# Attention product of two heads as one 512-column operand, and a later transpose step, in an encoder kernel on Trainium2

## Chip, cores, metric

One core of a Trainium2 chip runs the whole program in one launch. The metric is device time in microseconds (us). Three runs of the kernel before took 2294.6, 2294.95 and 2295.01 us, median 2294.95 us.

## What is computed

The reference is a two-layer encoder on 256 positions of width 2048, in float32. Layer 0 mixes tokens with mixer A, layer 1 with mixer B (dilated windows); each is followed by a gated MLP with a width-3 convolution. Everything that the change touches is in mixer A:

```python
qkv = h @ w_qkv                                   # h: 256 x 2048, RMS-normed
q = axial_rope(rms_norm(q, q_gain))               # 16 heads of 128
k = axial_rope(rms_norm(k, k_gain))               #  4 heads of 128
logits = einsum('bqkgd,bskd->bkgqs', q, k) * 128 ** -0.5
p = softmax(logits)
o = einsum('bkgqs,bskd->bqkgd', p, v)             # 4 query heads share one k/v head
return o @ w_o
```

## The kernel before

**Numbers.** Almost every product is made of three matmuls with fp32r operands. A float32 value is split into a high part, `hi`, and a rest, `lo`, and `mm3` (L205 to 212) adds hi by hi (L210), lo by hi (L211) and hi by lo (L212). `split` (L192 to 197) makes the pair: ScalarE (ACT) copies into `hi` (L196), VectorE (DVE) subtracts into `lo` (L197). Weights are split as they arrive: `wh` on ACT (L156), `wl` on DVE (L157), in tiles of 1024 columns.

**Projections and steps.** `project` computes a 512-column block of `h @ w` as four calls of `feed`, one for each 512 rows of the weight. A feed loads its weights over the SP queue (L134), and has two halves; each half has one cast `wh`, one cast `wl` and two k-tiles, and each k-tile issues six 512-column matmuls (L144 to 146). Work that belongs to an earlier block is hung in between as Python generators in the list `pending`. `feed` calls `step` after each k-tile: after the first of a half it goes on only with a generator that stopped at `yield "half"`, after the second with the first generator of the list. So one step of a generator is spent for each half of a feed, 8 for each `project`. The engine queues keep, for the most part, the order in which this Python code issues instructions, but the tool that schedules them takes whatever it reckons to be ready, and the weight casts run in a region of raised priority (`AHEAD`), ahead of their place.

**Mixer A.** First `project2` makes the k and v blocks. Then, for g = 0 to 3, `project` makes the q block of four heads and `start(attend(g, accs))` hangs in its attention, which runs during the next `project` (for g = 3 during `out_proj`). `attend` runs in this order:

- `qk_post` (L581): ACT copies the block to `s` (tile `stg`, L477) and squares it into `sq` (L591), GpSimd (POOL) makes the rotary half `t2` in four instructions (L597); one step later DVE multiplies by the cosines (L600), and at the next one adds `t2` into `ro` (L602), sums the squares (L603), and POOL takes the root (L273, tile `rqk`).
- one step later `heads_T` issues eight TensorE (PE) transposes of `ro` (L494) and two splits into `qT`.
- then k = 0 to 5, each a step in two parts around `yield "half"`. First part, for k < 4: the product of q and k of head k (six 256-column matmuls into a PSUM tile), its maximum (L646), the scaling of the maximum (L648), two exponentials on ACT (L652), a reciprocal (L655), and the scaling of the probabilities on POOL (L656, tile `pr`). Second part, for k = 1 to 4: four transposes of the probabilities of head k-1 (L665) and their split into `pTh`, `pTl`. Behind it, for k = 2 to 5: the product with v of head k-2, two k-tiles by three matmuls of 256 columns, and its split into the slot of the head (`ah`, `al`).

Tiles with the same tag share memory. `rp` and `gbs`, the rotary table and the two gains (loaded at L522 and L525, read by POOL at L530 and L534 for `ct` and `st`), lie in the buffers of `pTh` and `pTl`, which have two each.

`out_proj` runs `project2` over `w_ao`: the first three feeds of two column blocks, then `drain()`, then the last feed of each. The last feeds read the slots of g = 3.

Of the kernel before, what the change touches and what calls it, by code (L numbers as in the profile page):

```python
# [7 lines left out]
F32 = mybir.dt.float32  # L8
F32R = mybir.dt.float32r
# [4 lines left out]
P = 128  # L14
D = 2048
NT = 256
# [12 lines left out]
def tile_encoder(ctx: ExitStack, tc: tile.TileContext, x, xT, w_a, w_ao, q_gain, k_gain, w_b, w_bo,  # L29
# [26 lines left out]
    def nm(s):  # L56
        uid[0] += 1
        return f"{s}_{uid[0]}"

    def ps_tile():  # L60
        return psp.tile([P, 512], F32, tag="ps", name=nm("ps"))
# [3 lines left out]
    def copy(o, i):  # L65
        turn[0] ^= 1
        if turn[0]:
            nc.scalar.activation(o, i, AF.Copy)
        else:
            nc.vector.tensor_copy(o, i)  # L70
# [121 lines left out]
    def split(hi, lo, src):  # L192
        if lo is None:
            copy(hi, src)
            return
        nc.scalar.activation(hi, src, AF.Copy)  # L196
        nc.vector.tensor_tensor(lo, src, hi.bitcast(F32), ALU.subtract)  # L197
# [7 lines left out]
    def mm3(o, lhsT, rhs, ls, rs, start, stop):  # L205
        (lh, ll), (rh, rl) = lhsT, rhs
        if ll is None:
            nc.tensor.matmul(o, lh[ls], rh[rs], start=start, stop=stop)  # L208
            return
        nc.tensor.matmul(o, lh[ls], rh[rs], start=start, stop=False)  # L210
        nc.tensor.matmul(o, lh[ls], rl[rs], start=False, stop=False)  # L211
        nc.tensor.matmul(o, ll[ls], rh[rs], start=False, stop=stop)  # L212

    def pair_tile(pool, shape, tag, bufs=1, whole=False):
        if whole:
            return pool.tile(shape, F32, tag=tag + "h", name=nm(tag), bufs=bufs), None
        return tuple(pool.tile(shape, F32R, tag=tag + c, name=nm(tag + c), bufs=bufs) for c in "hl")
# [9 lines left out]
    def new_slots(kts):  # L227
        return {kt: new_slot(kt) for kt in kts}
# [251 lines left out]
    def evac_split(pool, accs, rstd, whole=False):  # L480
        hi, lo = pair_tile(pool, [P, 2, 512], "v", 1, whole)
        for m in range(2):
            split_scaled(hi[:, m, :], lo if lo is None else lo[:, m, :], accs[m], rstd[:, m:m + 1])
        return hi, lo

    def heads_T(o, s):
        for hp in range(2):
            if hp:
                yield
            t = ps_tile()  # L490
            for j in range(2):
                for m in range(2):
                    i = 2 * hp + j
                    nc.tensor.transpose(t[:, j * NT + m * P:j * NT + (m + 1) * P],  # L494
                                        s[:, m, i * P:(i + 1) * P], ident)
            hi, lo = (v[:, 2 * hp:2 * hp + 2, :].rearrange("p a c -> p (a c)") for v in o)
            split(hi, lo, t)
# [12 lines left out]
    def mixer_a():  # L510
        with tc.tile_pool(name="apool", bufs=1) as ap:
# [1 line left out]
            hT, ss_in = {}, new_ss()  # L513
            kgs = list(range(4))

            rp = ap.tile([P, 2, 2, P], F32, tag="pTh", name="rp", bufs=2)
            gbs = ap.tile([P, 4, P], F32, tag="pTl", name="gbs", bufs=2)
            tabs = {}
            rstd = []

# [61 lines left out]
            def qk_post(accs, which, keep, scale=1.0):  # L582
                s = evac_scaled(ap, accs, rstd[0], 1)
                ct, st = tabs[which]
                ssq = small.tile([P, 8], F32, tag="ssq", name=nm("ssq"))
                r = small.tile([P, 8], F32, tag="rqk", name=nm("rqk"), bufs=3)
                ro = ap.tile([P, 2, 512], F32, tag="ro", name=nm("ro"))
                t2 = ap.tile([P, 2, 512], F32, tag="t2", name=nm("t2"))
                sq = ap.tile([P, 2, 512], F32, tag="sq", name=nm("sq"))
                for m in range(2):  # L590
                    nc.scalar.activation(sq[:, m, :], accs[m], AF.Square, scale=rstd[0][:, m:m + 1])  # L591
                rv, sv = (t.rearrange("p m (a c) -> p m a c", a=4) for t in (ro, s))
                for m in range(2):
                    t5, s5 = (t[:, m, :].rearrange("p (a f e c) -> p a f e c", a=4, f=2, e=2) for t in (t2, s))
                    st5 = st[:, m, :].rearrange("p (f e c) -> p f e c", f=2, e=2)
                    for e in range(2):
                        nc.gpsimd.tensor_tensor(t5[:, :, :, e, :], s5[:, :, :, 1 - e, :],  # L597
                                                st5[:, None, :, e, :].to_broadcast([P, 4, 2, 32]), ALU.mult)
                yield
                nc.vector.tensor_tensor(rv, sv, ct[:, :, None, :].to_broadcast([P, 2, 4, P]), ALU.mult)  # L600
                yield
                nc.vector.tensor_tensor(ro, ro, t2, ALU.add)  # L602
                nc.vector.tensor_reduce(ssq, sq.rearrange("p m (a c) -> p (m a) c", a=4), axis=AX.X, op=ALU.add)  # L603
                rsqrt_mean(r, ssq, P * scale * scale, EPS / (scale * scale))
                keep.extend((ro, r))

            slots = new_slots(range(16))
# [15 lines left out]
            v = evac_split(ap, va, rstd[0])  # L623
# [3 lines left out]
            def attend(g, accs):  # L627
                keep = []
                yield from qk_post(accs, "q", keep, SCALE)
                ro, rq = keep  # L630
                rqv = rq.rearrange("p (m a) -> p m a", m=2)
                qT = pair_tile(ap, [P, 4, NT], "qT")
                yield
                for _ in heads_T(qT, ro):
                    pass
                prs, pTs, ots = {}, {}, {}
                for k in range(6):
                    yield
                    if k < 4:
                        i = k  # L640
                        s = ps_tile()
                        for m in range(2):
                            mm3(s[:, m * NT:(m + 1) * NT], qT, kT,
                                (slice(None), i, slice(m * P, (m + 1) * P)), (slice(None), g), True, True)
                        mx = small.tile([P, 2], F32, tag="mx", name=nm("mx"), bufs=3)
                        nc.vector.tensor_reduce(mx, s.rearrange("p (m c) -> p m c", m=2), axis=AX.X,  # L646
                                                op=ALU.max, negate=True)
                        nc.vector.tensor_tensor(mx, mx, rqv[:, :, i], ALU.mult)  # L648
                        pr = ap.tile([P, 2, NT], F32, tag="pr", name=nm("pr"), bufs=2)
                        l = small.tile([P, 2], F32, tag="l", name=nm("l"), bufs=3)  # L650
                        for m in range(2):
                            nc.scalar.activation(pr[:, m, :], s[:, m * NT:(m + 1) * NT], AF.Exp,  # L652
                                                 bias=mx[:, m:m + 1], scale=rq[:, 4 * m + i:4 * m + i + 1],
                                                 accum_out=l[:, m:m + 1])
                        nc.vector.reciprocal(l, l)  # L655
                        nc.gpsimd.tensor_tensor(pr, pr, l[:, :, None].to_broadcast([P, 2, NT]), ALU.mult)  # L656
                        prs[i] = pr
                    yield "half"
                    if 1 <= k < 5:
                        i = k - 1  # L660
                        pr = prs.pop(i)
                        t = ps_tile()
                        for m in range(2):
                            for kt in range(2):
                                nc.tensor.transpose(t[:, kt * NT + m * P:kt * NT + (m + 1) * P],  # L665
                                                    pr[:, m, kt * P:(kt + 1) * P], ident)
                        pTs[i] = pair_tile(ap, [P, 2 * NT], "pT", 2)
                        split(pTs[i][0], pTs[i][1], t)
                    if k >= 2:
                        i = k - 2  # L670
                        pT = pTs.pop(i)
                        ot = ps_tile()[:, :NT]
                        for kt in range(2):
                            mm3(ot, v, pT, (slice(None), kt, slice(g * P, (g + 1) * P)),
                                (slice(None), slice(kt * NT, (kt + 1) * NT)), kt == 0, kt == 1)
                        hi, lo = slots[4 * g + i]
                        split(hi, lo, ot)

            for g in range(4):
                start(attend(g, project(w_a, g, hT, kgs)))  # L680
# [258 lines left out]
```

## Time and profile before

| what | us |
|---|---|
| runs, median of three | 2294.95 |
| the profiled execution, its own time | 2294.99 |
| span of the profile (first to last instruction) | 2293.2 |
| PE busy | 2280.3 |
| DVE busy | 1631.3 |
| ACT busy | 1218.1 |
| POOL busy | 170.3 |

The busy time of PE counts a matmul to its modelled end, so that consecutive matmuls overlap; what a matmul costs is read from the distance between the starts of neighbours. `PEld` are PE's weight loads, which run beside the matmuls. In the timeline a row has the start, the duration, engine, line, operation, output and inputs, and in brackets the idle time of the engine before it and what ended it; consecutive alike instructions are merged into one row with their count. A row that ends in `x4` is thus four instructions.

### The profile page before, as it was taken

What the parts mean: (1) busy time and instruction counts of PE and PEld (TensorE: products, weight loads), DVE (VectorE), ACT (ScalarE), POOL (GpSimd) and SP (SyncE); (2) the same over time, 40 slices, a digit from 0 to 9 for tenths busy, and PEclk for the clock granted to TensorE, in tenths of its full rate; (3) what the DMA queues carried; (4) which work ended last, traced back from release to release, by engine and by line L of the source; (5) the groups of instructions that cost most, each with busy time, mean ns of one, the idle gap of its engine ahead of it and who ended that gap; (6) DMA issues with size and microseconds to landing.
All of it is one profiled execution on the core that took longest, in us unless ns stands there. A gap on an engine that the chain in (4) does not pass through costs nothing.

```text
span 2293.2 us, 31100 instructions
## 1 busy us (share of the span) xinstructions
PE 2280.3 (99%) x11641; PEld 1947.1 (85%) x11641; DVE 1631.3 (71%) x2284; ACT 1218.1 (53%) x1746; POOL 170.3 (7%) x170
## 2 busy tenths in 40 slices
PE   9999999999999999999999999999999999999998
PEld 7888888888888888888888888888888888888886
DVE  6877877776457776878866875676777744777754
ACT  7565565554345555545454554445555533555543
POOL 2331101110000000010000000000000000000010
PEclk9999999999999999999999999999999999999999
DMA  8535656765555555566555554566555565555554
GB/s 299 166 131 164 202 190 206 214 213 194 194 194 184 192 190 189 188 216 210 185 175 181 178 189 163 178 198 206 189 189 189 188 194 193 191 190 187 192 191 149
DMA packets 261447, 437.57 MB, mean 191 GB/s; under 512 B 17216, under 2 KB 198208, under 8 KB 261168
## 3 DMA queue, kind: packets, MB, share of 16 engines
q1 hardware_dynamic: 254912, 425.64, 56.6%
q0 software_dynamic: 5952, 9.38, 1.6%
q8 instruction: 91, 1.49, 0.3%
q10 hardware_dynamic: 432, 0.56, 0.1%
q14 instruction: 60, 0.49, 0.1%
HBM read 429.20 MB, written 6.29 MB: 190 GB/s over the span
## 4 chain that ended last, share of the span: by engine, by line
PE 97%; DVE 1%; DMA 0%; issue 0%; POOL 0%; ACT 0%; SPq 0%; POOLq 0%; DVEq 0%; ACTq 0%
PE acc L123 28%; PE acc L145 17%; PE acc L146 17%; PE acc L144 17%; PE acc L121 15%; PE ps L208 1%; PE ps L211 1%; PE ps L212 0%; PE ps L210 0%; DMA raw<-in_w_a_dram 0%; DVE wl L157 0%; PE ps L665 0%; PE ps L815 0%; DVE tT L237 0%; POOL t L597 0%
## 5 line engine op out<-in xcount | busy, mean ns | idle before, releaser
L157 DVE TENSOR_TENSOR wl<-raw,wh 128x1024 fp32r<-128x1024 f32 (+1 forms) x456 | 553.5, 1216 | 320.1 <-ACT wh L156 316.2
L156 ACT ACTIVATE wh<-raw 128x1024 fp32r<-128x1024 f32 (+1 forms) x456 | 475.0, 1045 | 514.5 <-PE acc L146 449.6
L123 PE MATMUL acc<-xh,wh 128*128 128x512 f32 x2816 | 674.2, 391 | 0.0
L123 PEld LDWEIGHTS acc<-xh,wh 128*128 128x128 f32 x2816 | 517.0, 188 | 99.9 <-DVE v L356 0.4
L112 DVE TENSOR_TENSOR wl<-raw,wh 128x1024 fp32r<-128x1024 f32 x352 | 457.9, 1301 | 196.6 <-ACT wh L111 196.6
L111 ACT ACTIVATE wh<-raw 128x1024 fp32r<-128x1024 f32 x352 | 372.0, 1058 | 208.4 <-issue 70.9
L144 PE MATMUL acc<-wh,ah 128*128 128x512 f32 x1024 | 399.3, 390 | 0.0
L145 PE MATMUL acc<-wl,ah 128*128 128x512 f32 x1024 | 398.8, 389 | 0.0
L146 PE MATMUL acc<-wh,al 128*128 128x512 f32 x1024 | 398.7, 389 | 0.0
L121 PEld LDWEIGHTS acc<-xh,wl 128*128 128x128 f32 x2816 | 361.8, 191 | 14.2
L121 PE MATMUL acc<-xh,wl 128*128 128x256 f32 x2816 | 366.7, 283 | 0.0
L144 PE MATMUL acc<-wh,xh 128*128 128x512 f32 x768 | 302.7, 395 | 1.9 <-ACT wh L156 1.9
L145 PE MATMUL acc<-wl,xh 128*128 128x512 f32 x768 | 300.0, 391 | 0.2 <-DVE wl L157 0.2
L146 PE MATMUL acc<-wh,xh 128*128 128x512 f32 x768 | 299.8, 390 | 0.0
L146 PEld LDWEIGHTS acc<-wh,al 128*128 128x128 f32 x1024 | 192.2, 188 | 40.0
L144 PEld LDWEIGHTS acc<-wh,ah 128*128 128x128 f32 x1024 | 192.3, 188 | 39.4
L145 PEld LDWEIGHTS acc<-wl,ah 128*128 128x128 f32 x1024 | 192.3, 188 | 39.3
L146 PEld LDWEIGHTS acc<-wh,xh 128*128 128x128 f32 x768 | 144.2, 188 | 30.4
L144 PEld LDWEIGHTS acc<-wh,xh 128*128 128x128 f32 x768 | 144.4, 188 | 30.0 <-ACT wh L156 2.3
L145 PEld LDWEIGHTS acc<-wl,xh 128*128 128x128 f32 x768 | 144.4, 188 | 27.8 <-DVE wl L157 0.5
L375 POOL TENSOR_TENSOR cv<-cg,cv 128x512 f32<-128x512 f32 x44 | 63.5, 1444 | 1101.9 <-DVE cv L367 1101.9
L355 ACT ACTIVATE v<-acc 128x256 f32<-128x256 f32 x176 | 65.8, 374 | 108.5 <-PE acc L123 108.5
(156 smaller groups left out, 1385.8 us busy)
## 6 DMA issues: line engine op xcount, KB each, us to landing
raw<-in_w_up_dram SPq DMA_DIRECT2D x352, 512.0 KB, 3.7
raw<-in_w_down_dram SPq DMA_DIRECT2D x176, 512.0 KB, 3.6
raw<-in_w_b_dram SPq DMA_DIRECT2D x144, 512.0 KB, 3.8
raw<-in_w_bo_dram SPq DMA_DIRECT2D x48, 512.0 KB, 3.6
raw<-in_w_a_dram SPq DMA_DIRECT2D x40, 512.0 KB, 4.3
raw<-in_w_ao_dram SPq DMA_DIRECT2D x32, 512.0 KB, 3.7
raw<-in_w_a_dram SPq DMA_DIRECT2D x16, 256.0 KB, 6.1
h<-in_x_dram SPq DMA_DIRECT2D x4, 512.0 KB, 7.9
```

The lines of the kernel that those rows point to most:

```text
L111: nc.scalar.activation(wh, rk, AF.Copy)
L112: nc.vector.tensor_tensor(wl, rk, wh.bitcast(F32), ALU.subtract)
L121: nc.tensor.matmul(acc[j][:, :NT], wl[:, kt, c], lhs[4 * kg + kt][0], start=st, stop=sp)
L123: nc.tensor.matmul(acc[j], wh[:, kt, c], lhs[4 * kg + kt][2], start=st, stop=sp)
L144: nc.tensor.matmul(accs[m], xh[:, c], wh[:, j, :], start=st, stop=False)
L145: nc.tensor.matmul(accs[m], xh[:, c], wl[:, j, :], start=False, stop=False)
L146: nc.tensor.matmul(accs[m], xl[:, c], wh[:, j, :], start=False, stop=sp)
L156: nc.scalar.activation(wh[:, c], r[:, c], AF.Copy)
L157: nc.vector.tensor_tensor(wl[:, c], r[:, c], wh[:, c].bitcast(F32), ALU.subtract)
L208: nc.tensor.matmul(o, lh[ls], rh[rs], start=start, stop=stop)
L355: nc.scalar.activation(v[:, j], acc[j][:, NT:], AF.Copy)
L375: nc.gpsimd.tensor_tensor(cv, cg, cv, ALU.mult)
```

## The change

Three things are changed in mixer A.

- The product with v is taken for two heads at a time. `pTh` and `pTl` become one tile of 128 x 2 x 2 x 256 for a pair of heads (one buffer each instead of two), head by head in the inner index, so that a k-tile of both heads is one operand of 512 columns. The product of heads 0 and 1 is issued at k = 3 and that of heads 2 and 3 at k = 5, ahead of that step's transposes, where it was behind them at k = 2 to 5. The two results are split one after the other.
- `attend(0)` has one more `yield` in front of `heads_T`.
- `rp` lies in the buffer of `sq`; `gbs` in the now single buffer of `pTl`.

```diff
-            rp = ap.tile([P, 2, 2, P], F32, tag="pTh", name="rp", bufs=2)
-            gbs = ap.tile([P, 4, P], F32, tag="pTl", name="gbs", bufs=2)
+            rp = ap.tile([P, 2, 2, P], F32, tag="sq", name="rp")
+            gbs = ap.tile([P, 4, P], F32, tag="pTl", name="gbs")
...
                 qT = pair_tile(ap, [P, 4, NT], "qT")
                 yield
+                if g == 0:
+                    yield
                 for _ in heads_T(qT, ro):
                     pass
-                prs, pTs, ots = {}, {}, {}
+                prs, pTs = {}, {}
...
                     yield "half"
+                    if k in (3, 5):
+                        i = k - 3
+                        pT = [p.rearrange("p k a c -> p k (a c)") for p in pTs.pop(i // 2)]
+                        ot = ps_tile()
+                        for kt in range(2):
+                            mm3(ot, v, pT, (slice(None), kt, slice(g * P, (g + 1) * P)),
+                                (slice(None), kt), kt == 0, kt == 1)
+                        for j in range(2):
+                            split(*slots[4 * g + i + j], ot[:, j * NT:(j + 1) * NT])
                     if 1 <= k < 5:
...
-                        pTs[i] = pair_tile(ap, [P, 2 * NT], "pT", 2)
-                        split(pTs[i][0], pTs[i][1], t)
-                    if k >= 2:
-                        i = k - 2
-                        pT = pTs.pop(i)
-                        ot = ps_tile()[:, :NT]
-                        for kt in range(2):
-                            mm3(ot, v, pT, (slice(None), kt, slice(g * P, (g + 1) * P)),
-                                (slice(None), slice(kt * NT, (kt + 1) * NT)), kt == 0, kt == 1)
-                        hi, lo = slots[4 * g + i]
-                        split(hi, lo, ot)
+                        if i % 2 == 0:
+                            pTs[i // 2] = [ap.tile([P, 2, 2, NT], F32R, tag="pT" + c, name=nm("pT" + c))
+                                           for c in "hl"]
+                        split(*(p[:, :, i % 2, :] for p in pTs[i // 2]), t.rearrange("p (k c) -> p k c", k=2))
```

## The prediction

> **What bounds the kernel now.** I read the page first: shares of the engines, the granted clock, the chain.
>
> ```profile
> span 2293.2 us, 31100 instructions
> PE 2280.3 (99%) x11641; PEld 1947.1 (85%) x11641; DVE 1631.3 (71%) x2284; ACT 1218.1 (53%) x1746; POOL 170.3 (7%) x170
> PEclk9999999999999999999999999999999999999999
> PE 97%; DVE 1%; DMA 0%; issue 0%; POOL 0%; ACT 0%; SPq 0%; POOLq 0%; DVEq 0%; ACTq 0%
> ```
>
> PE is the bound from end to end, at the full clock, and idle for only 12.9 us (2293.2 - 2280.3). The profiled execution took 2294.99 us, 1.8 us more than its span and 0.04 us more than the median of the runs; my sum is made against 2294.99.
>
> Next the busy times by stretch: from the k block's attention work to the end of mixer A's q blocks. The first column is the stretch, the second its length, the third PE busy with its count.
>
> ```profile
> 0.00:46.30 46.30, 42.77 (x181) 34.62 (x182) 29.04 (x45) 32.67 (x59) 9.32 (x24) 1.00 0.92 322
> 46.30:73.30 27.00, 27.00 (x121) 22.36 (x120) 24.10 (x34) 13.99 (x16) 6.49 (x5) 1.00 0.57 183
> 73.30:103.40 30.10, 29.53 (x157) 24.92 (x156) 23.96 (x34) 19.42 (x38) 11.17 (x8) 1.00 0.56 180
> 103.40:133.90 30.50, 30.50 (x169) 25.96 (x169) 23.18 (x34) 19.38 (x39) 10.46 (x9) 1.00 0.43 140
> 164.50:200.00 35.50, 35.50 (x196) 30.08 (x195) 25.84 (x38) 22.37 (x42) 11.51 (x10) 1.00 0.42 136
> ```
>
> The attention runs between about 82 and 200 us. In all of it PE stands still once, for 0.57 us (30.10 - 29.53). So there is little to win from waits; what else the change can win must come from matmuls becoming cheaper or fewer. Since DVE (24 of 30 us) and ACT (19 of 30) are well filled, what it can lose is a wait that it opens.
>
> **The one wait.** The timeline around it, PE first, then DVE and POOL, which set it:
>
> ```profile
> 71.68 0.39 PE L146 MATMUL acc<-wh,xh 128*128 128x512 f32 x1
> ...
> 81.88 0.39 PE L146 MATMUL acc<-wh,xh 128*128 128x512 f32 x1
> 82.84 1.09 PE L494 MATMUL ps<-ident,ro 128*128 128x128 f32 x8 [0.57 <-DVE ro L602]
> 83.69 0.47 PE L144 MATMUL acc<-wh,xh 128*128 128x512 f32 x1
> ...
> 75.06 5.51 POOL L597 TENSOR_TENSOR t<-stg,st_q 128x256 f32<-128x256 f32 x4 [16.66 <-ACT stg L477]
> 78.63 3.02 DVE L157 TENSOR_TENSOR wl<-raw,wh 128x1024 fp32r<-128x1024 f32 x2
> 81.57 1.21 DVE L602 TENSOR_TENSOR ro<-ro,t 128x1024 f32<-128x1024 f32 x1
> 85.06 1.27 DVE L197 TENSOR_TENSOR qTl<-ps,qTh 128x512 fp32r<-128x512 f32 x2
> 86.54 0.28 PE L210 MATMUL ps<-kTh,qTh 128*128 128x256 f32 x1
> ```
>
> From 71.68 to 81.88 lie 45 matmuls of 512 columns, 0.227 us apart. The first q block's transposes then start 0.96 us after their neighbour, 0.73 more than that: they wait for `ro`, ready at 82.78. PE loses 0.73 us here (the bracket counts 0.57, since it counts the neighbour to its modelled end).
>
> With the extra yield in `attend(0)` the transposes come half a feed later: 12 matmuls, 2.7 us, so at 82.11 + 2.7 = 84.8 us. `ro` is then 2.0 us old. **Gain 0.73 us**; bounds 0 (if the DVE subtraction of two tiles, 3.02 us, slides once more in front of L602) and 0.73. What is late next: both `qTl` end at 86.33, and the first q by k product starts at 86.54. All of that moves along with the transposes, so it keeps its distance of a half feed. The sums and the small root on POOL (L273) and the casts of weights stay where they were and are covered by the same matmuls. The extra step moves no DMA. Every later step of all four attentions comes one half feed later, g = 1 to 3 because `attend(g)` is served only when `attend(g-1)` has ended.
>
> **The product with v.** One product as it stands without transposes in front of it, and one behind transposes:
>
> ```profile
> 96.04 0.60 PE L665 MATMUL ps<-ident,pr 128*128 128x128 f32 x4
> 96.39 0.36 PE L210 MATMUL ps<-pTh,vh 128*128 128x256 f32 x1
> 96.59 0.28 PE L211 MATMUL ps<-pTl,vh 128*128 128x256 f32 x1
> ...
> 97.19 0.39 PE L144 MATMUL acc<-wh,xh 128*128 128x512 f32 x1
> 98.58 0.28 PE L210 MATMUL ps<-kTh,qTh 128*128 128x256 f32 x1
> ...
> 108.56 0.28 PE L210 MATMUL ps<-pTh,vh 128*128 128x256 f32 x1
> ...
> 109.28 0.39 PE L144 MATMUL acc<-wh,xh 128*128 128x512 f32 x1
> ```
>
> From 108.56 to 109.28 six matmuls of 256 columns take 0.72 us, 0.120 each. Behind transposes the six take 0.80 (96.39 to 97.19); the first is 0.20 instead of 0.12 long. That 0.08 us belongs to the change from transposes to products: at 83.69, where a projection follows transposes, its first matmul is longer by as much (0.47 modelled against the 0.39 of its like). The number of such changes stays (16 transposes of probabilities, each followed by something), so nothing is won or lost there.
>
> A pair of heads costs 12 x 0.120 = 1.44 us before. After, six matmuls of 512 columns: at 0.227 (the quiet rows above) 1.36 us, at the 0.232 of the six between 97.19 and 98.58, 1.39 us. Eight pairs: gain 0.64 or 0.40 us. I take 0.5, between them, as the new matmuls lie amid attention, nearer to the second. The columns streamed are the same; what goes is 48 matmuls and 48 weight loads, with about 0.012 us of overhead each. **Gain 0.5 us.**
>
> The Trainium skill has a lower value for this term: in "TensorE: Matmul & The Clock Gate", section "Back-to-back issue gap", a warm matmul of N columns costs N/2.4 + 2.5 ns alone. By that, as an estimate from its figures, two of 256 columns cost 218.3 ns and one of 512 215.8, so 48 merged pairs would win only 0.12 us, and the sum would be about 2293.9. The trace does not agree: its rows say 0.120 and 0.227 us, and they decide.
>
> **The rest of the merge.** The splits of probabilities write 256 of every 512 columns, and the two results are split at k = 3 and 5 instead of one at each of k = 2 to 5: same number and width, all on ACT and DVE. I cost them at nothing, since what needs them comes late: a `pTl` that ends at 102.70 (`102.01` below) goes with a product behind the transposes of 104.60, 2.3 us later, and a pair's second `pTl` keeps this distance of half a feed. With one buffer the split of head 2 must wait until the pair's product has read the tile, but the transposes that it waits for anyhow stand behind that product on PE. Were the cover gone, one `pTl` split late would cost its 0.69 us, at most, for each of eight pairs.
>
> `rp` in the buffer of `sq` puts a wait in front of the first `sq` on ACT, with the `wh` casts behind it. It has long been met:
>
> ```profile
> 29.43 0.77 POOL L534 TENSOR_TENSOR st_q<-rp,gbs 128x64 f32<-128x64 f32 x1
> ...
> 48.48 1.26 ACT L591 ACTIVATE sq<-acc,rstd 128x512 f32<-128x512 f32 x2
> ```
>
> The last reader ends at 30.2, `sq` is first written at 48.5. The loads of `rp` and `gbs` keep their place on the SP queue and write a buffer nobody used before them. Cost 0.
>
> **What moves over a block's end.** This is where a new wait could come. Now the end of block 1 (about 103.2 us) falls behind the last head's q by k product; after, that product is the first thing behind the end, since all is half a feed later. The rows of head 3 and of the next block's start:
>
> ```profile
> 99.18 0.28 PE L212 MATMUL ps<-kTh,qTl 128*128 128x256 f32 x1
> ...
> 104.60 0.66 PE L665 MATMUL ps<-ident,pr 128*128 128x128 f32 x4
> ...
> 100.10 1.21 DVE L157 TENSOR_TENSOR wl<-raw,wh 128x1024 fp32r<-128x1024 f32 x1
> 102.01 0.69 DVE L197 TENSOR_TENSOR pTl<-ps,pTh 128x512 fp32r<-128x512 f32 x1 [0.62 <-ACT pTh L196]
> 104.53 1.78 DVE L600 TENSOR_TENSOR ro<-stg,ct_q 128x1024 f32<-128x1024 f32 x1 [0.73 <-ACT stg L477]
> ...
> 103.50 1.04 POOL L656 TENSOR_TENSOR pr<-pr,l 128x512 f32<-128x512 f32 x1 [3.73 <-PE acc L146]
> 104.50 3.80 POOL L597 TENSOR_TENSOR t<-stg,st_q 128x256 f32<-128x256 f32 x4
> ...
> 103.22 1.28 ACT L477 ACTIVATE stg<-acc,rstd 128x512 f32<-128x512 f32 x2
> ```
>
> From the end of the q by k product (99.30) to the scaled probabilities (103.50 + 1.04 = 104.54) the chain of head 3 takes 5.24 us, and its transposes start at 104.60: just in time, even a little late, as four take 0.66 instead of 0.60 us. After the change, counted from the block's end T: product of head 3 0.72, k-tile 1.38 (the six above), product of heads 0 and 1 1.38, transposes of head 2 0.44, k-tile 1.38, k-tile 1.38: the transposes of head 3 start at T + 6.68, their probabilities are ready at T + 0.72 + 5.24 = T + 5.96. Slack 0.7 instead of none. Head 2's transposes start behind the pair's product at T + 3.48; its q by k product ended at T - 3.2 (two k-tiles and one set of transposes before T), so it is ready at T + 2.0. Heads 0 and 1 keep the gaps that they have. So the small delays of the last head go: **gain 0.06 a block, 0.2 us in all**, bounds 0 and 0.3.
>
> In `out_proj`, attention of g = 3 ends in the first k-tile of the sixth feed, ahead of `drain`; its last slots are read two k-tiles into the seventh, five k-tiles (6.9 us) later. Cost 0.
>
> **The sum.** 0.73 + 0.5 + 0.2 = 1.4 us less: 2294.99 - 1.4 = 2293.6 us. Its own bounds are the least of each term (0 + 0.4 + 0) and the most (0.73 + 0.64 + 0.3): 2294.6 and 2293.3.
>
> **Rivals.**
>
> *POOL's order at the block's end (slower).* The four `t2` instructions of the next block (3.80 us on POOL) become ready at T + 0.75, when ACT has copied the first half (1.28 for two). The scaling of head 2's probabilities becomes ready at about T + 0.9, one `pr` (1.04) ahead of T + 2.0. If the four stand first in POOL's queue, it starts at T + 4.55, ends at T + 5.6, and PE's transposes at T + 3.48 wait 2.1 us, three times (there is no next block after g = 3): 6.4 us, so 2293.6 + 6.4 = 2300.0. It decides from the second `t2` ahead: one (0.95) still ends at T + 2.9. For it: the schedule takes what is ready, and now `t2` follows L656 at once (104.50). Against it: head 2's scaling is issued half a feed earlier and is reckoned ready at the same time. 5%.
>
> *DVE's order there.* If the multiplication L600 (1.78 us) slips into head 3's chain beside the cast (1.21) that is in it already, head 3 is ready at T + 7.74, 1.06 late, three times 3.2 us: 2296.8. For it: DVE takes L600 as soon as `stg` is there (104.53). Against: the maximum's scaling has precedence once it is ready. 13%.
>
> *The steady pitch.* The matmuls of a projection amid attention go at up to 0.232 against 0.227 us. If small matmuls cause that, fewer of them could free up to half of 0.005 us on about 370 matmuls, 0.9 us more: 2292.7. For it, the two rows; against, the transposes and the q by k products stay. 9%.
>
> *The change doesn't do what it says.* The merged matmul costs twice 0.120 us after all, as nothing here shows a 512-column one with `pTh` as input: 2293.6 + 0.5 = 2294.1; or the wait for `ro` only moves along: 2293.6 + 0.73 = 2294.3. Against it, 0.232 is the longest distance that the rows of 512 columns show without a switch. 10%. The formula of the Trainium skill's page that is named above points to the first of the two.
>
> **How the numbers follow.** The forecast has 61%, the rest is as above, with 2% for something unseen, as much up as down. A change within 0.2% (4.6 us) is about what a measurement of this kernel can't tell from none. Forecast, pitch, no gain and DVE's order all lie within it: 61 + 9 + 10 + 13 = 93%. Slower by more needs POOL's order or the unseen: 6%. Faster by more would need over three times all that the trace shows to be had: 1%. The range 2292.5 to 2296.8 leaves out POOL's order, the unseen and a part of DVE's order.
>
> **What would show it.** Right: no idle PE in front of the first q block's transposes (L494); six 512-column matmuls in 1.36 to 1.39 us with `pTh`, `pTl` as inputs, 48 fewer matmuls; the transposes of head 3 four in 0.60 us. Wrong: PE idle in front of L665 with POOL `pr` as releaser and L597 rows just ahead of L656 on POOL; or L600 between L646 and L648 on DVE behind a block's end. Wrong altogether would be a time that moved outside of 72 to 215 us, since beyond that no instruction is touched.

## The result, and the profile after

The changed kernel takes 2298.47 us (median of 21 runs, 2297.75 to 2299.58) against 2294.88 us before (21 runs, 2293.96 to 2295.57): ratio 1.0016, 95% interval 1.001 to 1.0022. It is 3.6 us slower; 1.4 us less were forecast, and the range ended at 2296.8. The span of the profiled execution is 2296.3 us, 3.1 more than before.

Page of the changed kernel, the span, the busy times and the chain by engine:

```profile
span 2296.3 us, 31009 instructions
PE 2281.6 (99%) x11593; PEld 1945.0 (85%) x11593; DVE 1634.6 (71%) x2284; ACT 1217.8 (53%) x1746; POOL 174.9 (8%) x170
PE 98%; POOL 1%; DVE 1%; issue 0%; DMA 0%; ACT 0%; SPq 0%; POOLq 0%; DVEq 0%
```

48 matmuls are gone, as announced. POOL, at 0% of the chain before, has 1% of it: something on POOL now ends last. Where, the busy times by stretch say (stretch, length, PE busy with its count), each stretch about one q block:

```profile
73.30:100.40 27.10, 27.10 (x140) 22.90 (x139) 22.60 (x28) 17.16 (x31) 10.12 (x7) 1.00 0.60 197
100.40:132.40 32.00, 31.01 (x159) 25.40 (x159) 23.97 (x35) 19.50 (x39) 11.42 (x9) 1.00 0.40 131
132.40:164.40 32.00, 30.81 (x158) 25.24 (x157) 24.20 (x35) 19.61 (x39) 11.42 (x9) 1.00 0.41 134
164.40:203.00 38.60, 37.63 (x192) 30.95 (x191) 28.68 (x43) 23.77 (x48) 13.50 (x11) 1.00 0.41 132
```

The idle 0.57 us of the first block is gone. In its place PE stands still for about 1 us in each of the three that follow a block's end. The list of waits of the changed kernel, from 46 to 230 us (total, times, longest), names what for:

```profile
PE ps L676 <- POOL pr L658: 2.9, 3, 1.1
PEld ps L211 <- DVE pTl L197: 1.6, 3, 0.5
```

L676 are the transposes of the probabilities, L658 is their scaling (`pr`) on POOL; a head's maximum is L648 in the changed kernel, its scaling L650, the exponentials L654 and the reciprocal L657. The timeline of the first of the three waits, PE, then POOL, DVE and ACT:

```profile
84.82 1.03 PE L494 MATMUL ps<-ident,ro 128*128 128x128 f32 x8
...
101.86 0.39 PE L210 MATMUL ps<-pTh,vh 128*128 128x512 f32 x1
...
103.23 0.60 PE L676 MATMUL ps<-ident,pr 128*128 128x128 f32 x4
...
106.18 0.39 PE L146 MATMUL acc<-wh,xh 128*128 128x512 f32 x1
107.47 0.66 PE L676 MATMUL ps<-ident,pr 128*128 128x128 f32 x4 [0.90 <-POOL pr L658]
...
110.74 0.39 PE L210 MATMUL ps<-pTh,vh 128*128 128x512 f32 x1
111.22 0.50 PE L211 MATMUL ps<-pTl,vh 128*128 128x512 f32 x1
111.56 0.39 PE L212 MATMUL ps<-pTh,vl 128*128 128x512 f32 x1
...
100.62 1.04 POOL L658 TENSOR_TENSOR pr<-pr,l 128x512 f32<-128x512 f32 x1 [2.98 <-PE ps L212]
101.62 4.79 POOL L597 TENSOR_TENSOR t<-stg,st_q 128x256 f32<-128x256 f32 x4
106.38 1.03 POOL L658 TENSOR_TENSOR pr<-pr,l 128x512 f32<-128x512 f32 x1
...
100.67 0.69 DVE L648 TENSOR_REDUCE mx<-ps 128x2 f32<-128x512 f32 x1 [0.21 <-PE ps L212]
101.45 1.30 DVE L600 TENSOR_TENSOR ro<-stg,ct_q 128x1024 f32<-128x1024 f32 x1
102.67 0.69 DVE L650 TENSOR_TENSOR mx<-mx,rqk 128x2 f32<-128x2 f32 x1
103.29 1.21 DVE L603 TENSOR_REDUCE ssq<-sq 128x8 f32<-128x1024 f32 x1
104.42 1.39 DVE L157 TENSOR_TENSOR wl<-raw,wh 128x1024 fp32r<-128x1024 f32 x1
105.73 0.15 DVE L657 RECIPROCAL l<-l 128x2 f32<-128x2 f32 x1
105.81 0.40 DVE L197 TENSOR_TENSOR al<-ps,ah 128x256 fp32r<-128x256 f32 x1
106.45 2.05 DVE L602 TENSOR_TENSOR ro<-ro,t 128x1024 f32<-128x1024 f32 x1 [0.24 <-POOL t L597]
...
110.49 0.68 DVE L197 TENSOR_TENSOR pTl<-ps,pTh 128x512 fp32r<-128x512 f32 x1
...
104.49 0.20 ACT L654 ACTIVATION_READ_ACCUMULATOR pr<-ps,mx,rqk 128x1 f32 x1
```

Head 3's transposes start 1.29 us after the matmul ahead of them (106.18 to 107.47), where 0.23 is usual: 1.06 us lost. Its probabilities were scaled on POOL at 106.38, right behind the four L597 of the next block, which began at 101.62 and took 4.79 us. But the reciprocal that POOL also needs came only at 105.73: between it and the maximum (100.67) DVE had put L600, L603 and a weight cast, all work of the next block or the next weights. The exponentials had ended on ACT at 104.69, so it was DVE that held the reciprocal. So two engines were late at once, POOL until 106.4 and DVE until 105.9. Further on, the pair's product loses 0.36 us (0.48 and 0.34 between its first three starts, where 0.46 for both together is usual in a product that meets no wait), since `pTl` of head 3 comes only at 110.49, behind L602, which took 2.05 us, the `pTl` of head 2 and a weight cast.

At the other two block ends the same places lose 1.24 and 1.03, and 0.38 and 0.37 us. All together: 1.06 + 1.24 + 1.03 + 0.36 + 0.38 + 0.37 = 4.44 us.

### The profile page after: what moved, and what is told of

Same layout as the page of the kernel before. It is cut to its first block, busy times and chain, and to the rows that moved or that the text cites. A ratio compares the mean times of both kernels' runs of the same rounds, so it can differ in the third digit from the quotient of the medians.

```text
span 2296.3 us, 31009 instructions
## 1 busy us (share of the span) xinstructions
PE 2281.6 (99%) x11593; PEld 1945.0 (85%) x11593; DVE 1634.6 (71%) x2284; ACT 1217.8 (53%) x1746; POOL 174.9 (8%) x170
## 4 chain that ended last, share of the span: by engine, by line
PE 98%; POOL 1%; DVE 1%; issue 0%; DMA 0%; ACT 0%; SPq 0%; POOLq 0%; DVEq 0%
PE acc L123 28%; PE acc L145 17%; PE acc L146 17%; PE acc L144 17%; PE acc L121 15%; POOL t L597 1%; PE ps L208 1%; PE ps L211 0%; PE ps L212 0%; PE ps L210 0%; PE ps L819 0%; DMA raw<-in_w_a_dram 0%; PE ps L676 0%; DVE wl L157 0%; PE ps L494 0%
```

## Experiments

The stretch that the change touches runs from the first matmul of q block 0 to the first of the MLP. It is read from the starts of these two in each trace; the median is that of the runs. The kernel before took 2294.63 us beside e1, e2, e4 and e6, and 2294.67 beside the others (33 runs each).

| kernel | first matmul of q block 0 | first of the MLP | stretch | against before | median, us |
|---|---|---|---|---|---|
| before | 52.19 | 262.09 | 209.90 | | 2294.88 |
| changed | 52.17 | 265.24 | 213.07 | +3.17 | 2298.47 |
| e1, merge only | 52.27 | 261.88 | 209.61 | -0.29 | 2294.97 |
| e2, later step only | 51.95 | 265.32 | 213.37 | +3.47 | 2298.46 |
| e4, t2 held back | 51.52 | 260.08 | 208.56 | -1.34 | 2293.68 |
| e6, L600 held back | 52.04 | 260.40 | 208.36 | -1.54 | 2293.55 |
| e5, both held back | 52.68 | 260.98 | 208.30 | -1.60 | 2293.69 |
| e9, both, without merge | 51.97 | 260.71 | 208.74 | -1.16 | 2293.76 |
| e7, L600 with one input | 53.01 | 264.30 | 211.29 | +1.39 | 2296.37 |
| e3, ACT scales head 3 | 52.14 | 262.50 | 210.36 | +0.46 | 2296.44 |

My theory after the result: the extra step, not the merge, puts head 3's softmax across the block's end, among the next block's work. First, the two parts alone.

**e1, the merge without the extra step.**

```diff
                 yield
-                if g == 0:
-                    yield
                 for _ in heads_T(qT, ro):
```

> The changed kernel without the extra yield in attend(0): product for two heads and new buffers, but every attention step where it was before. Theory (the half feed of delay puts the last head's softmax chain across the block's end, where POOL and DVE take up the next block's work first): no idle PE before the transposes of head 3, four of them in about 0.60 us; the wait of the first q block (0.73 us) is back; time 0.5 us under the kernel before, about 2294.4. Rival (the merge itself costs, by one buffer for a pair or by two splits in a row): the three waits of about 1 us before L676 and the 0.35 us inside the product of heads 2 and 3 stay, time about 2298.

Median 2294.97 us, ratio to before 1.0002 (0.9993 to 1.0011): no difference that can be told. PE waits in its trace:

```profile
PE ps L494 <- DVE ro L602: 0.6, 1, 0.6
PEld ps L211 <- DVE pTl L197: 0.9, 3, 0.3
```

No wait before the transposes of head 3; the old wait of the first q block is back. By the stretch only 0.3 of the 0.5 us arrive; the pair's product still meets `pTl` late, by 0.10 to 0.16 us at each block's end. The rival falls: the merge does not make the loss.

**e2, the extra step without the merge** (the kernel before with the two lines `if g == 0: yield`).

> The kernel before with nothing but the extra yield in attend(0). Theory (the delay does it): the wait of the first q block goes (-0.73 us) and three waits before the transposes of head 3 come. The product of heads 0 and 1 is not in front here, so those transposes are asked for 0.6 us earlier than in the changed kernel, and each wait is 1.5 us or more: 4.5 or more in all, time about 2298.5 to 2300. Rival (merge costs): time 2294.2, as only the gain is left.

Median 2298.46 us, ratio 1.0016 (1.0007 to 1.0025): all of the loss. The list of waits:

```profile
PE ps L667 <- POOL pr L658: 3.9, 3, 1.4
```

Three waits (1.37, 1.59 and 1.36 us by the starts), longer than in the changed kernel, as the pair's product does not stand in front of these transposes. That is the theory's mechanism and sign; of the 1.5 us or more for each wait that were written only one is reached, and the time lies just under the low end. POOL and DVE at the first block's end say which engine came last:

```profile
101.41 3.81 POOL L597 TENSOR_TENSOR t<-stg,st_q 128x256 f32<-128x256 f32 x4
106.55 1.04 POOL L658 TENSOR_TENSOR pr<-pr,l 128x512 f32<-128x512 f32 x1 [1.33 <-DVE l L657]
...
101.17 0.69 DVE L648 TENSOR_REDUCE mx<-ps 128x2 f32<-128x512 f32 x1 [0.40 <-PE ps L212]
...
106.23 0.15 DVE L657 RECIPROCAL l<-l 128x2 f32<-128x2 f32 x1
```

POOL is done with the four L597 at 105.22 and waits 1.33 us for the reciprocal, which comes 5.06 us after the maximum, just as in the changed kernel (100.67 to 105.73). So here the wait is DVE's. In the changed kernel, too, `pr` could have started only 0.32 us behind the reciprocal, at 106.05, had POOL been free; reckoned so, about 0.7 of the first 1.06 us is DVE's lateness, and POOL's adds the rest.

**e4 and e6: which of the two engines?** Both give the odd heads' `pr` a tag of its own and let one tile of `qk_post` share its buffer, so that the next block can write it only when head 3's transposes have read theirs. In e4 that tile is `t2` (POOL's L597), in e6 `ro` (DVE's L600).

```diff
-                        pr = ap.tile([P, 2, NT], F32, tag="pr", name=nm("pr"), bufs=2)
+                        pr = ap.tile([P, 2, NT], F32, tag=("pr", "t2")[i % 2], name=nm("pr"))
```

(e4; in e6 `"ro"` stands for `"t2"`.) The orders on PE are those of the changed kernel in both. In e4 the next block's sum L602 also comes later on DVE. In e6 not L600 alone is out of the way: L603 and the weight cast fall behind the reciprocal as well, and on ACT the exponentials go ahead of the weight cast.

> The changed kernel with t2 in the buffer of the odd heads' pr, so that the four L597 instructions of the next block can start only when the transposes of head 3 have read theirs; the orders on PE and ACT are the same as in the changed kernel, on DVE only what adds t2 moves back. If POOL's order holds head 3: pr starts at once after the reciprocal, the three waits before L676 go from 1.1 to between 0 and 0.5 us, the 0.35 us inside the product of heads 2 and 3 goes too since L602 is out of its way, time 2294 to 2296. If DVE's order holds it (L600, L603 and a weight cast between head 3's maximum and its reciprocal): the waits shrink by no more than 0.5 us each, time 2296.5 to 2298.

> The changed kernel with ro in the buffer of the odd heads' pr, so that L600 can start only after the transposes of head 3; POOL's and PE's orders are the same as in the changed kernel, on DVE the reciprocal of head 3 comes directly behind its scaled maximum, on ACT its exponentials come ahead of a weight cast. If POOL's order holds head 3: pr still starts when the four L597 are over, waits of 0.5 to 1.1 us each stay, time 2296.5 to 2298. If DVE's order holds it: the reciprocal is 1 us or more earlier, the waits go, time about 2294.5.

Medians 2293.68 us for e4 (ratio 0.9995, 0.9986 to 1.0003) and 2293.55 for e6 (0.9994, 0.9985 to 1.0003). Neither has idle PE from the first q block to the end of mixer A. Taken singly, e4 reads as its first sentence (POOL's order) and e6 as its second (DVE's), and both times are a little under what was written. Together they say something else: each of the two alone removes all of the loss, so neither engine's order makes head 3 late by itself. How that can be shows in the timelines. e4, POOL and DVE:

```profile
104.67 1.04 POOL L658 TENSOR_TENSOR pr<-pr,l 128x512 f32<-128x512 f32 x1 [3.66 <-PE acc L146]
...
100.01 0.69 DVE L648 TENSOR_REDUCE mx<-ps 128x2 f32<-128x512 f32 x1 [0.21 <-PE ps L212]
100.80 1.30 DVE L600 TENSOR_TENSOR ro<-stg,ct_q 128x1024 f32<-128x1024 f32 x1
102.02 0.15 DVE L650 TENSOR_TENSOR mx<-mx,rqk 128x2 f32<-128x2 f32 x1
102.09 1.21 DVE L603 TENSOR_REDUCE ssq<-sq 128x8 f32<-128x1024 f32 x1
103.22 1.21 DVE L157 TENSOR_TENSOR wl<-raw,wh 128x1024 fp32r<-128x1024 f32 x1
104.35 0.15 DVE L657 RECIPROCAL l<-l 128x2 f32<-128x2 f32 x1
```

e6, POOL and DVE:

```profile
101.49 2.84 POOL L597 TENSOR_TENSOR t<-stg,st_q 128x256 f32<-128x256 f32 x4
104.27 1.06 POOL L658 TENSOR_TENSOR pr<-pr,l 128x512 f32<-128x512 f32 x1
...
100.55 0.69 DVE L648 TENSOR_REDUCE mx<-ps 128x2 f32<-128x512 f32 x1 [0.23 <-PE ps L212]
101.27 0.28 DVE L650 TENSOR_TENSOR mx<-mx,rqk 128x2 f32<-128x2 f32 x1
103.05 0.17 DVE L657 RECIPROCAL l<-l 128x2 f32<-128x2 f32 x1 [1.50 <-ACT pr L654]
```

In e4 DVE has the same four instructions between maximum and reciprocal as the changed kernel, and yet needs 4.34 us (100.01 to 104.35) and not 5.06 (100.67 to 105.73): the scaling of the maximum takes 0.15 instead of 0.69, the cast 1.21 instead of 1.39. In e6 POOL has the four L597 ahead of head 3 as in the changed kernel, and they take 2.84 and not 4.79 us. Each engine runs slower while the other has its part of the next block. For transposes in time `pr` must start at most 4.7 us after the start of the maximum (in the changed kernel 106.41, where PE was free, less 1.04 for `pr` itself, less 100.67). It starts at 4.66 in e4, at 3.72 in e6, and at 5.71 in the changed kernel. So DVE's order alone uses up nearly all the room (0.04 us is left in e4), and what makes it late in the changed kernel is the time that the two take from each other.

**e7: is it the two slowing each other?** L600 is exchanged for an instruction that reads one tile of SBUF instead of two, so the multiplication of q by the cosines is left out. The orders on all engines stay.

```diff
-                nc.vector.tensor_tensor(rv, sv, ct[:, :, None, :].to_broadcast([P, 2, 4, P]), ALU.mult)
+                if which == "k":
+                    nc.vector.tensor_tensor(rv, sv, ct[:, :, None, :].to_broadcast([P, 2, 4, P]), ALU.mult)
+                else:
+                    nc.vector.tensor_reduce(ro, s[:, :, :, None], axis=AX.X, op=ALU.add)
```

> The changed kernel with L600 of the q blocks as a tensor_reduce over a last axis of one, which copies: the multiplication by the cosines is left out. The orders on all engines are those of the changed kernel; only L600 reads one tile of SBUF instead of two. Theory (POOL's t2 and DVE's instructions with two SBUF inputs shut each other out, and this is what makes head 3 late): the first of the four L597 behind a block's end takes 0.74 us instead of 1.72, the scaling of the maximum 0.15 instead of 0.69, pr of head 3 starts about 1 us earlier, the waits of 1.06 to 1.24 us go to 0 or 0.2, time about 2293.7. Rival (the orders alone make it late): the waits stay above 0.7 us each, time above 2297.

Median 2296.37 us, ratio 1.0009 (1.0 to 1.0018). POOL and DVE of its timeline at the first block's end (L661, L603, L653 and L660 are L658, L600, L650 and L657 of the changed kernel):

```profile
102.46 2.83 POOL L597 TENSOR_TENSOR t<-stg,st_q 128x256 f32<-128x256 f32 x4
106.62 1.04 POOL L661 TENSOR_TENSOR pr<-pr,l 128x512 f32<-128x512 f32 x1 [1.33 <-DVE l L660]
...
101.49 0.69 DVE L651 TENSOR_REDUCE mx<-ps 128x2 f32<-128x512 f32 x1 [0.21 <-PE ps L212]
102.28 1.22 DVE L603 TENSOR_REDUCE ro<-stg 128x1024 f32<-128x1024 f32 x1
103.42 0.51 DVE L653 TENSOR_TENSOR mx<-mx,rqk 128x2 f32<-128x2 f32 x1
...
104.98 1.40 DVE L157 TENSOR_TENSOR wl<-raw,wh 128x1024 fp32r<-128x1024 f32 x1
106.30 0.15 DVE L660 RECIPROCAL l<-l 128x2 f32<-128x2 f32 x1
```

The four L597 take 2.83 us again, in the same place and order: what stretched them to 4.79 was their neighbours on DVE with two inputs in SBUF, L600 first of all, the only one exchanged. POOL is free at 105.3 and now waits 1.33 us for the reciprocal. That has hardly come earlier (4.81 us after the maximum), for DVE still loses to POOL's reads: 0.51 instead of 0.15, 1.40 instead of 1.21. The waits shrink to 0.48, 0.66 and 0.44 us, halfway, so both sentences that were written miss: this one exchange takes away about half of the wait, and the 0.35 to 0.38 us in each product of the second pair stay. If I take the DVE losses off as well (0.36 + 0.19), the reciprocal comes 4.26 us after the maximum, which would be in time. This last step is reckoned; the run nearest to it is e4, where the same DVE order without L597 beside it needs 4.34 us.

**e3, ACT scales head 3** instead of POOL, with two activations (`scale=l`); all else as in the changed kernel.

```diff
+                        if i == 3:
+                            for m in range(2):
+                                nc.scalar.activation(pr[:, m, :], pr[:, m, :], AF.Copy, scale=l[:, m:m + 1])
+                        else:
+                            nc.gpsimd.tensor_tensor(pr, pr, l[:, :, None].to_broadcast([P, 2, NT]), ALU.mult)
```

> The changed kernel with the scaling of head 3's probabilities on ACT instead of POOL; DVE's order is unchanged, POOL still does t2 at the same place and still meets L600. The reciprocal of head 3 then sets the time (105.9 in the changed kernel, where pr starts at 106.4), and ACT needs two instructions of about 0.45 us: waits of 0.4 to 0.7 us instead of 1.06 to 1.24, time 2295.5 to 2297. If POOL's order were the whole reason: waits of 0.2 or less, time about 2294.

Median 2296.44 us, ratio 1.0008 (0.9998 to 1.0017). The time is in the range, for another reason than the one written. Its reciprocal comes at 105.71, ACT takes 0.91 us for both halves where POOL takes 1.04, and PE starts on the first half while ACT does the second: only about 0.12 us is lost in each set of transposes, less than the 0.4 that was written. What remains is 0.33 to 0.36 us in the pair's product, three times, behind the same late `pTl`. The median lies 1.8 us above before, the stretch 0.5; 0.7 of the difference is a longer tail behind the last matmul in its profiled execution, the rest I can't place.

**e5 and e9, both held back, with the merge and without.** `ro` and `t2` become one tile in the buffer of the odd heads' `pr`, in the changed kernel (e5) and in e2 (e9).

```diff
-                ro = ap.tile([P, 2, 512], F32, tag="ro", name=nm("ro"))
-                t2 = ap.tile([P, 2, 512], F32, tag="t2", name=nm("t2"))
+                rt = ap.tile([P, 2, 2, 512], F32, tag="rt", name=nm("rt"))
+                ro, t2 = rt[:, 0], rt[:, 1]
...
-                        pr = ap.tile([P, 2, NT], F32, tag="pr", name=nm("pr"), bufs=2)
+                        pr = ap.tile([P, 2, NT], F32, tag=("pr", "rt")[i % 2], name=nm("pr"))
```

> The changed kernel with ro and t2 in one tile, in the buffer of the odd heads' pr: both L597 and L600 of the next block wait for the transposes of head 3. If the lateness needs both orders at once, and each of the two kernels with one of them removed has already won all there is: the same as these, 2293.3 to 2293.8, no idle PE in mixer A. If each has left a part: 2292.5 or less.

> The kernel before with the extra yield and with ro and t2 held back as in e5, but the product with v head by head. What is left is the gain of the later transposes: 0.73 us under the kernel before, 2293.9; the difference to e5 is the merge, forecast as 0.5 us. If the merge wins nothing, it equals e5.

Medians 2293.69 (ratio 0.9997, 0.9988 to 1.0006) and 2293.76 (0.9996, 0.9987 to 1.0005). e5 wins nothing over e4 and e6: with either obstacle gone there is nothing left to win. By the stretch e9 lies 1.16 us under before and e5 another 0.44 under e9: the gains of the later step and of the merge without the loss, from one trace of each. The step's 1.16 is more than the 0.73 and 0.2 that were forecast for it; whether holding back adds something of its own, no run separates. In the medians 0.07 us between them can't be told from nothing.

e4, e5 and e6 have medians 0.95 to 1.1 us under the kernel before, and stretches 1.3 to 1.6 shorter. They keep the change and lose its cost; the intervals of their ratios still hold 1, so that they beat the kernel before is likely by the traces and not proven by the runs.

## Why the prediction was wrong

- **The wait for `ro`: right.** The transposes of the first q block start at 84.82 (84.8 forecast) with no idle time.
- **The merged product: right.** Where nothing stalls it, six matmuls of 512 columns take 1.37 us (101.86 to 103.23; 1.36 to 1.39 forecast). By the stretch the merge is worth 0.44 us (e9 to e5, one trace of each; 0.5 forecast), which the medians neither show nor deny.
- **The sum of gains: right.** 1.4 us forecast; by the stretch 1.34 to 1.60 in the three kernels that have the change without its loss, by the medians 0.95 to 1.1. "The change doesn't do what it says" falls with the rows of the transposes and the product. "The steady pitch" has nothing for it either: the six matmuls of a k-tile amid the attention still take 1.39 us, from the end of a q by k product at 100.47 to 101.86, 0.232 each.
- **"What moves over a block's end": this step failed.** It said that the chain of head 3 takes 5.24 us and that its transposes, asked for at T + 6.68, have 0.7 us of slack, a gain of 0.2 us. The moment was right: they were asked for at 106.41, with T at 99.75 (T + 6.66). The chain was not: from the end of its q by k product at 100.47 to the end of `pr` at 107.41 it took 6.94 us, where 5.94 would have been in time. With one of the two engines cleared it took 5.90 (e4) and 4.99 us (e6). I took 5.24 us from a row of another place, where the next block's work on DVE and POOL began only after head 3 had passed, and carried it unchanged to one where that work runs beside it.
- **The rivals had the pieces, each alone.** DVE's order came as described, L600 between the maximum and its scaling; the 1.06 us that it was given per block is what was measured at the first, but by luck: it is the length of one L600 less the slack, and L600 with all of DVE's order does not make the delay alone (e4). POOL's four L597 came first too, though ahead of head 3 and not of head 2 (100.62, 101.62), and alone they make no delay either (e6). Each was priced by itself, with 18% for both together, and with lengths from rows in which they had already met once (104.50 and 104.53: L597 3.80, L600 1.78 us), taken as fixed. What decided was that both run beside head 3's chain: on DVE L650 takes 0.69 instead of 0.15 us and the cast 1.39 instead of 1.21, on POOL the four L597 4.79 instead of 2.83.
- **A term put at nothing:** `pTl` of head 3 came late, 0.36 to 0.38 us in each product of the second pair, 1.11 of the 4.44 us. I costed the two later `pTl` at nothing, as they kept their half feed of distance; but DVE had L602 in front of them. That L602 was stretched to 2.05 us is not needed for it: in e3 it takes 1.23, and the product still loses 0.33 to 0.36.
- **What a measurement can tell: set too wide.** I held that a change of up to 4.6 us is about what can't be told from none; 21 runs of each kernel told 3.6 us from nothing.

The account: 4.44 us of new waits, and 0.06 us in each of the three sets of transposes behind them (0.66 us for four instead of 0.60), are 4.62 us. Less the 1.34 to 1.60 us that the kernels without the loss gain, that leaves 3.0 to 3.3; the stretch shows 3.17.

## What to carry to other kernels

A chain's duration read from a trace belongs to the company it had there: when a step moves across a boundary, list what each engine will have in its queue beside it, and price the chain anew. Work that a scheduler starts early because it is ready can be kept back by a buffer that it must share with the critical tile; here that cost no instruction. Test each suspect alone: two causes that each seem to account for the whole wait may both be needed for it.

## What the runs showed of the hardware

In these traces a GpSimd instruction and a VectorE instruction with two inputs in SBUF shut each other out for their whole length. The rows that group L597 of the q blocks from 100 us on (count, then shortest, median and longest in ns), of the kernel before and of the changed kernel:

```profile
L597 POOL TENSOR_TENSOR t<-stg,st_q x12: 730/737/1730, 104.5 to 168.6; 128x256 f32<-128x256 f32 x12
L597 POOL TENSOR_TENSOR t<-stg,st_q x12: 728/1230/1726, 101.6 to 168.6; 128x256 f32<-128x256 f32 x12
```

An instruction of 0.73 us has a second duration of 1.73, which three of the twelve have before and six in the changed kernel, with none between. The long ones are those that fall on a running L600 or weight cast, which read two tiles in SBUF, as the first of the four at 101.62 falls on L600 (101.45 to 102.75); beside L603, a reduction with one input, they keep 0.73 us, and in e7, where L600 is such a reduction, all twelve behind a block's end do. In turn L650, a product of 128 x 2 elements, waits up to 0.54 us for POOL to finish. And L602 takes 2.05 us in the changed kernel, where POOL scales head 3 beside it (106.38 to 107.41), but 1.23 in e3, where ACT does the scaling.

This is what the Trainium skill says in "SBUF — State Buffer", section "Who interferes with whom": a VectorE instruction with two inputs in SBUF and a GpSimd instruction that reads SBUF need the same port, and the later one waits until the other has ended, while a reduction never takes part. The traces agree, with 1.0 us lost by POOL and 0.54 by DVE as above. The rows of before showed it already, as L597 of 0.73 and 1.73 us; my sum took their total of 3.80 us as a constant.
